# An MLP in two phases, with the down projection as seven products of combined quarters

## The chip, the core and the metric

The kernel runs on one NeuronCore of a Trainium2 chip. TensorE multiplies matrices, VectorE and ScalarE work element by element, GpSimd does almost nothing here, and SyncE (SP) issues nearly all DMAs, in order, to 16 DMA engines. Each engine works through its own queue in order and waits on semaphores of the others. The metric is the device time of one execution in microseconds (us). The median of three runs before is 2216.18 us (2214.98 to 2216.64).

## What is computed

One decoder layer over 512 tokens of width 2048: token mixing, cross-attention, then a squared-ReLU MLP with hidden width 8192, and a final RMSNorm. The change touches the last two:

```python
hn = rmsnorm(h, norm_mlp_g[l])
h = h + jnp.einsum('blf,fd->bld', jnp.square(jax.nn.relu(jnp.einsum('bld,df->blf', hn, w_up[l]))), w_down[l])
...
return rmsnorm(h, norm_final_g)
```

All inputs are float32.

## The kernel before

Activations lie transposed: a tile holds 128 channels on partitions and the 512 tokens along the row. The residual `h` is 16 such tiles, `hres`. Each float32 product is made of three TensorE products of a shorter float type: an operand x is split into xh (ScalarE copies it with rounding) and xl = x - xh (VectorE subtracts), and `mm3` adds wh xh, wh xl and wl xh into one PSUM bank.

`wload` fetches eight 128x128 weight blocks by one DMA into `wr` (two buffers) and splits them into `wh` and `wl` (three buffers each). `gemm` runs `mm3` over these blocks. In all of this the weight block is the stationary operand (128x128) and the activations move (512 columns).

The MLP runs over eight chunks of 1024 hidden channels. In a chunk eight up tiles are made (16 blocks deep; VectorE applies ReLU and the norm's factor, ScalarE squares, `split` makes `uh` and `ul`). Then 16 output tiles of down are made, each eight blocks deep, and VectorE adds each to its tile of `hres`. Per chunk this is 8 x 16 x 3 = 384 matmuls up and 16 x 8 x 3 = 384 matmuls down.

At the end the squares of `hres` are summed over partitions on TensorE, `rsqrt` runs eleven small VectorE instructions, the result is spread over partitions on TensorE, and 16 scalings on VectorE are followed by 16 writes of the output.

A scheduler sets the order on each engine from the program's order and from priorities; what stands inside `urgent()` comes as early as its inputs allow in the scheduler's reckoning. The pools' buffers decide when a load may start: a DMA into a buffer waits for the last reader of what was in it.

Of the kernel before, what the change touches and what calls it, by code (L numbers as in the profile page):

```python
# [56 lines left out]
def trunk(ctx, tc, A, out):  # L57
# [866 lines left out]

    pd = pool("mlp", side="left", reuse_waits="tile")
    for f in range(0, DFF // P, FC):
        UH, UL = [], []
        for j in range(FC):
            o = psum_mm()
            gemm(o, A["w_up"][f + j], list(range(KT)), XH_, XL_)  # L930
            with urgent():
                r = pd.tile([P, L], F32, name="r", bufs=2)
                V.scalar_tensor_tensor(r, o, 0.0, rsh2, op0=OP.max, op1=OP.mult)  # L933
                S.activation(r, r, AF.Square)  # L934
                h, l = split(r, f"uh{j}", f"ul{j}", pd, [P, L])
            UH.append(h)
            UL.append(l)
# [7 lines left out]
    o = rs_psum(sumsq(hres), 1.0 / D, EPS)  # L945
    for c in range(KT):
        t = pd.tile([P, L], F32, name="ot", bufs=4)
        V.scalar_tensor_tensor(t, hres[c], vc("fin_g", c), o, op0=OP.mult, op1=OP.mult)
        Q.dma_start(out[:, c], t)

# [84 lines left out]
```

## Time and profile before

| | before |
|---|---|
| median of three runs | 2216.18 us |
| the profiled execution's own time | 2214.54 us |
| its span, first to last instruction | 2212.8 us |
| TensorE busy | 2169.6 us, 98% |
| VectorE busy | 1168.3 us, 53% |
| ScalarE busy | 778.2 us, 35% |
| DMA, mean | 110 GB/s |
| mean granted clock of TensorE | 0.994 of 2.4 GHz |

Busy time of TensorE counts overlapping matmuls once, and says that something was in flight, not how fast. What a matmul costs is read from the starts of successive ones. The chain of waits goes back from the last instruction, at each step to what released it. In the views by line, a line that helpers use (`mm3`, `split`, `wload`) holds the work of several stages, which the tile names tell apart.

### The profile page before, as it was taken

How to read it: one execution, taken by the hardware profiler on the slowest of the kernel's cores; microseconds unless marked ns; L12 is line 12 of the kernel's file. 1: busy time of each engine (PE TensorE's matmuls, PEld its weight loads, DVE VectorE, ACT ScalarE, POOL GpSimd, SP SyncE). 2: the span in 40 equal slices, each digit the busy share in tenths (PEclk: the TensorE clock that was granted, in tenths of full speed). 3: DMA queues.
4: the chain of work that ended last, by engine and by line, in shares of the span. 5: the costliest groups of instructions: out<-in, count | busy, mean ns of one | idle time of the engine just before them, and what ended most of it. 6: DMA issues, size and time to landing. Idle time of an engine off the chain costs nothing.

```text
span 2212.8 us, 24813 instructions
## 1 busy us (share of the span) xinstructions
PE 2169.6 (98%) x9672; PEld 1757.9 (79%) x9672; DVE 1168.3 (53%) x1761; ACT 778.2 (35%) x1131; POOL 18.1 (1%) x57
## 2 busy tenths in 40 slices
PE   8999999999999999999999999999999999999996
PEld 6777777656988788888888888888888888888885
DVE  7999999976766663333333333333333333333344
ACT  6565543546435543222223212222212222222231
POOL 0000000000000000000000000000000000000000
PEclk9999999999999999999999999999999999999998
DMA  8553326433433133323332333332332332332332
GB/s 295 169 164 122 111 78 213 132 92 100 145 100 105 48 119 96 95 95 98 101 98 95 96 95 99 100 97 96 96 96 98 101 97 96 95 96 99 101 96 95
DMA packets 82134, 244.40 MB, mean 110 GB/s; under 512 B 10448, under 2 KB 12112, under 8 KB 82016
## 3 DMA queue, kind: packets, MB, share of 16 engines
q1 hardware_dynamic: 79808, 235.47, 33.7%
q0 software_dynamic: 2208, 7.34, 0.9%
q8 instruction: 76, 1.25, 0.2%
q14 instruction: 42, 0.34, 0.0%
HBM read 229.12 MB, written 13.13 MB: 109 GB/s over the span
## 4 chain that ended last, share of the span: by engine, by line
PE 92%; DMA 3%; DVE 3%; ACT 1%; issue 1%; SPq 0%; ACTq 0%; DVEq 0%
PE mm L129 29%; PE mm L131 29%; PE mm L130 29%; PE acc L480 1%; PE acc L791 1%; PE two L762 1%; DMA wr<-in_w_xk 1%; DVE wl L125 1%; PE sm L786 1%; DVE al L151 1%; ACT wh L124 0%; DMA ss<-in_pool_w 0%; DVE hc L540 0%; DMA sB<-in_xtok 0%; PE two L422 0%
## 5 line engine op out<-in xcount | busy, mean ns | idle before, releaser
L124 ACT ACTIVATE wh<-wr 128x1024 fp32r<-128x1024 f32 (+1 forms) x424 | 411.7, 971 | 1235.0 <-PE mm L130 1146.0
L129 PE MATMUL mm<-ah,wh 128*128 128x512 f32 (+1 forms) x1920 | 742.9, 387 | 5.3 <-ACT cs L438 2.4
L131 PE MATMUL mm<-ah,wl 128*128 128x512 f32 (+1 forms) x1920 | 741.8, 387 | 0.2 <-DVE wl L125 0.2
L130 PE MATMUL mm<-al,wh 128*128 128x512 f32 (+1 forms) x1920 | 740.1, 385 | 0.0
L125 DVE TENSOR_TENSOR wl<-wr,wh 128x1024 fp32r<-128x1024 f32 (+1 forms) x424 | 471.4, 1113 | 303.6 <-ACT wh L124 300.9
L129 PEld LDWEIGHTS mm<-ah,wh 128*128 128x128 f32 x1920 | 361.8, 188 | 83.0 <-issue 5.4
L131 PEld LDWEIGHTS mm<-ah,wl 128*128 128x128 f32 x1920 | 361.6, 188 | 76.7 <-issue 4.7
L130 PEld LDWEIGHTS mm<-al,wh 128*128 128x128 f32 x1920 | 361.9, 188 | 74.1 <-issue 5.4
L129 PE MATMUL mm<-uh,wh 128*128 128x512 f32 x1024 | 398.8, 389 | 0.0
L130 PE MATMUL mm<-ul,wh 128*128 128x512 f32 x1024 | 397.5, 389 | 0.0
L131 PE MATMUL mm<-uh,wl 128*128 128x512 f32 x1024 | 397.5, 389 | 0.0
L942 DVE TENSOR_TENSOR h<-mm,h 128x512 f32<-128x512 f32 x128 | 88.5, 692 | 415.9 <-PE mm L131 415.9
L131 PEld LDWEIGHTS mm<-uh,wl 128*128 128x128 f32 x1024 | 192.3, 188 | 39.8
L130 PEld LDWEIGHTS mm<-ul,wh 128*128 128x128 f32 x1024 | 192.3, 188 | 39.8
L129 PEld LDWEIGHTS mm<-uh,wh 128*128 128x128 f32 x1024 | 192.4, 188 | 39.7
L933 DVE SCALAR_TENSOR_TENSOR r<-mm,rsx 128x512 f32<-128x512 f32 x64 | 44.3, 692 | 208.7 <-PE mm L131 207.9
L540 DVE SCALAR_TENSOR_TENSOR hc<-pad,wdw,hc 128x512 f32<-128x512 f32 x120 | 86.1, 746 | 0.0
L723 DVE TENSOR_TENSOR h<-mm,h 128x512 f32<-128x512 f32 x64 | 43.9, 688 | 32.4 <-PE mm L131 31.8
L146 DVE TENSOR_TENSOR ul<-r,uh 128x512 fp32r<-128x512 f32 x64 | 44.3, 693 | 1.4 <-ACT uh L145 1.4
L188 DVE TENSOR_TENSOR sqa<-sqa,sqt 128x512 f32<-128x512 f32 x60 | 41.1, 685 | 5.0 <-ACT sqt L187 4.9
L145 ACT ACTIVATE uh<-r 128x512 fp32r<-128x512 f32 x64 | 40.5, 633 | 2.1
L934 ACT ACTIVATE r<-r 128x512 f32<-128x512 f32 x64 | 39.5, 618 | 0.8 <-DVE r L933 0.8
(305 smaller groups left out, 1166.9 us busy)
## 6 DMA issues: line engine op xcount, KB each, us to landing
wr<-in_w_up SPq DMA_DIRECT2D x128, 512.0 KB, 3.7
wr<-in_w_down SPq DMA_DIRECT2D x128, 512.0 KB, 3.7
wr<-in_w_in SPq DMA_DIRECT2D x56, 512.0 KB, 3.9
wr<-in_w_out SPq DMA_DIRECT2D x64, 256.0 KB, 3.0
h<-in_xT SPq DMA_DIRECT2D x16, 256.0 KB, 6.2
wr<-in_w_xk SPq DMA_DIRECT2D x8, 512.0 KB, 3.8
wr<-in_w_xv SPq DMA_DIRECT2D x8, 512.0 KB, 3.7
wr<-in_w_xq SPq DMA_DIRECT2D x8, 512.0 KB, 3.8
```

What stands on the lines that cost most here:

```text
L124: S.activation(h, r, AF.Copy)
L125: V.tensor_tensor(l, r, h.bitcast(F32), op=OP.subtract)
L129: T.matmul(o, wh, xh, start=start, stop=False)
L130: T.matmul(o, wh, xl, start=False, stop=False)
L131: T.matmul(o, wl, xh, start=False, stop=stop)
L145: S.activation(h, src, AF.Copy)
L146: V.tensor_tensor(l, src, h.bitcast(F32), op=OP.subtract)
L188: V.tensor_tensor(acc, acc, sq, op=OP.add)
L540: V.scalar_tensor_tensor(hc[c], hps[c][:, o:o + L], w, hc[c], op0=OP.mult, op1=OP.add)
L723: V.tensor_tensor(hres[c], o, hres[c], op=OP.add)
L933: V.scalar_tensor_tensor(r, o, 0.0, rsh2, op0=OP.max, op1=OP.mult)
L942: V.tensor_tensor(hres[c], o, hres[c], op=OP.add)
```

## The change

The MLP now has two phases: all 64 up tiles first, then all of down. Down uses a scheme with seven products in place of eight for 2x2 blocks (Strassen's, in Winograd's form). In a chunk of 1024 hidden channels the activations are a matrix of 512 tokens by 1024, cut into four quarters of 256 x 512, and the weights a matrix of 1024 x 2048, cut into four quarters of 512 x 1024. Four of the seven activation operands and four of the seven weight operands are sums or differences of quarters.

- `up_pair` makes two up tiles, builds the combinations of their quarters in `z` (seven operands, four of them made by VectorE), splits all seven at once and writes them to DRAM (`ud`). The residual is transposed to tokens on partitions (`h_block`, 64 transposes on TensorE), and four of the seven accumulators start from it (`xd`, also by way of DRAM).
- `down_product` loads one of the seven activation operands (`u_load`, three buffers), makes combinations of weight quarters in place where needed (line 1025), splits them into `w2h` and `w2l` (lines 1027 and 1028, five buffers each), and runs 48 matmuls in four tiles of twelve. Now the tokens are the stationary operand and the weights move. Results go into four PSUM banks, two sets in turn, and VectorE adds them to one of seven accumulators `x1` to `x7` in SBUF (line 1048).
- Weight quarters arrive as two tiles of 128x2048 each (`raw2`, eight buffers, one chunk's worth).
- In the last chunk `merge` forms the outputs from the accumulators, and `down_tail` norms them along the row. The output is written as tokens by channels.

```diff
-    for f in range(0, DFF // P, FC):
-        UH, UL = [], []
-        for j in range(FC):
-            o = psum_mm()
-            gemm(o, A["w_up"][f + j], list(range(KT)), XH_, XL_)
...
-        for c in range(KT):
-            o = psum_mm()
-            gemm(o, A["w_down"][c][:, f:f + FC], list(range(FC)), UH, UL)
             with urgent():
-                V.tensor_tensor(hres[c], o, hres[c], op=OP.add)
...
+    for j in range(2):
+        sl = slice(j * L, (j + 1) * L)
+        for b in range(2):
+            xs = pz.tile([P, 8, 256], F32, name="z", bufs=2).rearrange("p a n -> p (a n)")
+            x2, x3, x4, x7 = (xs[:, i * L:(i + 1) * L] for i in range(4))
+            S.activation(x2, h_block(b, 0, j), AF.Copy)
+            S.activation(x3, h_block(b, 1, j), AF.Copy, scale=-1.0)
+            S.activation(x7, h_block(b + 2, 1, j), AF.Copy)
+            V.tensor_tensor(x4, x7, h_block(b + 2, 0, j), op=OP.subtract)
+            for i, x in ((2, x2), (3, x3), (4, x4), (7, x7)):
+                Q.dma_start(xd[i, b][:, sl], x)
...
+    def up_pair(q, pr):
+        z = pz.tile([P, 8, 256], F32, name="z", bufs=2)
+        for i in range(2):
+            o = psum_mm()
+            gemm(o, A["w_up"][8 * q + 2 * pr + i], list(range(KT)), XH_, XL_)
+            with urgent():
+                r = pz.tile([P, L], F32, name="r", bufs=2)
+                V.scalar_tensor_tensor(r, o, 0.0, rsh2, op0=OP.max, op1=OP.mult)
+                S.activation(z[:, 1:3] if i else z[:, 0:8:7], r.rearrange("p (a b) -> p a b", a=2), AF.Square)
+        with urgent():
+            V.tensor_tensor(z[:, 3], z[:, 7], z[:, 2], op=OP.add)
+            V.tensor_tensor(z[:, 4], z[:, 3], z[:, 0], op=OP.subtract)
+            V.tensor_tensor(z[:, 5], z[:, 0], z[:, 7], op=OP.subtract)
+            V.tensor_tensor(z[:, 6], z[:, 4], z[:, 1], op=OP.subtract)
+            h, l = split(z[:, :7], "zh", "zl", pz, [P, 7, 256], bufs=2)
+            for i, t in enumerate((h, l)):
+                if pr == 0:
+                    ud[q, i] = dr.tile([P, 7, 4, 256], F32, name=f"ud{q}{i}")
+                Q.dma_start(ud[q, i][:, :, pr], t.bitcast(F32))
...
+            uu = u_load(q, idx)
+            wt = {}
+            for j in range(2):
+                for a in range(2):
+                    r = [x[j][:, 2 * a:2 * a + 2] for x in (w,) + tuple(t for c in comb for t in c)]
+                    for c in range(0, len(r) - 1, 3):
+                        V.tensor_tensor(flat(r[c + 1]), flat(r[c + 2]), flat(r[c + 3]), op=OP.subtract)
+                    h, l = w_tile("h"), w_tile("l")
+                    S.activation(flat(h), flat(r[0]), AF.Copy)
+                    V.tensor_tensor(flat(l), flat(r[0]), flat(h).bitcast(F32), op=OP.subtract)
+                    wt[j, a] = h, l
+        o = psum_two() + [psum_sm(), psum_sm()] if sets[0] else [psum_mm(), psum_mm(), psum_mm(), psum_acc()]
...
+            for p in range(2):
+                uh, ul = (t[:, 2 * a + p, b * P:(b + 1) * P] for t in uu)
+                T.matmul(o[2 * j + b], uh, h[:, p], start=a == 0 and p == 0, stop=False)
+                T.matmul(o[2 * j + b], uh, l[:, p], start=False, stop=False)
+                T.matmul(o[2 * j + b], ul, h[:, p], start=False, stop=a == 1 and p == 1)
...
+                        V.tensor_tensor(x, x, o[2 * j + b], op=OP.add)
...
+        down_product(q, 6, b22, (), (3,))
...
+        down_product(q, 0, b11, (), (1,))
+        down_product(q, 4, b22, ((b12, b12, b11), (b22, b22, b12)), (6,))
+        if last:
+            merge(2, 2, 1, OP.add)
+            merge(6, 6, 1, OP.add)
...
+        down_product(q, 5, b11, ((b11, b22, b11),), (7,))
...
+        down_product(q, 2, b22, ((b22, b22, b21),), (4,))
...
+        down_product(q, 3, b12, (), (3, 7) if last else (5,))
...
+        down_product(q, 1, b21, (), (2,), last)
```

Three places in the order of the instructions. On VectorE, inside the MLP of before, a split of weights and an accumulation of a finished output tile take turns:

```order
L125 TENSOR_TENSOR wl<-wr,wh 128x1024 [waits DMAHW3_49,Activation_49]
L942 TENSOR_TENSOR h_3412<-mm,h_3412 128x512 [waits PE_49]
L125 TENSOR_TENSOR wl<-wr,wh 128x1024 [waits DMAHW4_49,Activation_49]
L942 TENSOR_TENSOR h_3414<-mm,h_3414 128x512 [waits PE_49]
L125 TENSOR_TENSOR wl<-wr,wh 128x1024 [waits DMAHW5_49,Activation_49]
L942 TENSOR_TENSOR h_3416<-mm,h_3416 128x512 [waits PE_49]
```

On VectorE after the change, at the start of the second down chunk (`wq_12436` and `wq_12438` are its weight tiles for the first product, `wq_12444` a quarter already combined once for the third, `x_11961` the accumulator of the last product of the chunk before):

```order
L1028 TENSOR_TENSOR w2l<-wq_12436,w2h 128x1024 [waits DMAHW2_49,PE_49,Activation_49]
L1025 TENSOR_TENSOR wq_12436<-wq_12436,wq_12444 128x1024 [waits DVE_49]
L1028 TENSOR_TENSOR w2l<-wq_12436,w2h 128x1024 [waits Activation_49]
L1048 TENSOR_TENSOR x_11961<-x_11961,two 128x512 [waits PE_49] x2
L1025 TENSOR_TENSOR wq_12436<-wq_12436,wq_12444 128x1024 [waits DVE_49]
L1028 TENSOR_TENSOR w2l<-wq_12438,w2h 128x1024 [waits DMAHW5_49,Activation_49]
L1025 TENSOR_TENSOR wq_12438<-wq_12438,wq_12446 128x1024 [waits DVE_49]
```

The accumulation of a finished product now stands between splits and combinations for a later one, and the combinations are new.

On VectorE at the change from up to down: the last rows of an up stage before, ahead of the first accumulation of down (`r` is the eviction of an up tile, `ul` its low part):

```order
L933 SCALAR_TENSOR_TENSOR r<-mm,rsx 128x512 [waits DVE_49,PE_49]
L125 TENSOR_TENSOR wl<-wr,wh 128x1024 [waits DMAHW6_49,DVE_49,Activation_49]
L146 TENSOR_TENSOR ul_9910<-r,uh_9909 128x512 [waits Activation_49]
L942 TENSOR_TENSOR h_3386<-mm,h_3386 128x512 [waits PE_49]
L125 TENSOR_TENSOR wl<-wr,wh 128x1024 [waits DMAHW7_49,DVE_49,Activation_49]
```

and after, at the one place where the phase changes:

```order
L961 SCALAR_TENSOR_TENSOR r<-mm,rsx 128x512 [waits PE_49]
L964 TENSOR_TENSOR z<-z 128x256 [waits Activation_49]
L965 TENSOR_TENSOR z<-z 128x256 [waits DVE_49]
L967 TENSOR_TENSOR z<-z 128x256 [waits DVE_49]
L147 TENSOR_TENSOR zl<-z,zh 128x1792 [waits DMAHW2_49,Activation_49]
L1028 TENSOR_TENSOR w2l<-wq_11865,w2h 128x1024 [waits Activation_49]
```

Before, the weights of the first down tiles are split ahead of the last up tile's eviction or soon behind it; now the first split of down stands behind all work on the last pair of up tiles.

On SP, before, the loads of `w_down` follow those of `w_up` and wait for nothing but their two buffers:

```order
L119 DMA wr<-in_w_up 128x1024 [waits DMAHW0_49,DVE_49]
L119 DMA wr<-in_w_up 128x1024 [waits DMAHW1_49,DVE_49]
L119 DMA wr<-in_w_down 128x1024 [waits DMAHW2_49,DVE_49]
L119 DMA wr<-in_w_down 128x1024 [waits DMAHW3_49,DVE_49]
L119 DMA wr<-in_w_down 128x1024 [waits DMAHW4_49,DVE_49]
```

and after, at the change of phase (`wq_11873` to `wq_11879` are two of the four weight quarters, `u_11964` and `u_11966` the activations of the second product):

```order
L972 DMA ud_11428<-zh 896x1x256 [waits Activation_49]
L972 DMA ud_11430<-zl 896x1x256 [waits DMAHW1_49,DVE_49]
L1077 DMA wq_11873<-in_w_down 128x2048 [waits DMAHW2_49,PE_49]
L1077 DMA wq_11875<-in_w_down 128x2048 [waits PE_49]
L1077 DMA wq_11877<-in_w_down 128x2048 [waits DMAHW4_49,PE_49]
L1077 DMA wq_11879<-in_w_down 128x2048 [waits DMAHW5_49,PE_49]
L1010 DMA u_11964<-ud_7522 128x1024 [waits DMAHW7_49,DMAHW6_49,DMAHW0_49]
L1010 DMA u_11966<-ud_7524 128x1024
```

The four quarter tiles and the second product's activations stand behind the last write of the up phase. The first product's weights and activations (`wq_11865` to `wq_11871`, `u_11881`) are loaded earlier, in the up phase.

## Rows read from the trace of the kernel before

**Rows 1.** The page: span, busy time (share) by engine, chain of waits.

```profile
span 2212.8 us, 24813 instructions
PE 2169.6 (98%) x9672; PEld 1757.9 (79%) x9672; DVE 1168.3 (53%) x1761; ACT 778.2 (35%) x1131; POOL 18.1 (1%) x57
...
PE 92%; DMA 3%; DVE 3%; ACT 1%; issue 1%; SPq 0%; ACTq 0%; DVEq 0%
PE mm L129 29%; PE mm L131 29%; PE mm L130 29%; PE acc L480 1%; PE acc L791 1%; PE two L762 1%; DMA wr<-in_w_xk 1%; DVE wl L125 1%; PE sm L786 1%; DVE al L151 1%; ACT wh L124 0%; DMA ss<-in_pool_w 0%; DVE hc L540 0%; DMA sB<-in_xtok 0%; PE two L422 0%
```

**Rows 2.** MLP windows: us, busy PE, PEld, DVE, ACT, POOL; granted clock, DMA share, GB/s.

```profile
1000.00:1100.00 100.00, 100.00 (x443) 82.88 (x442) 35.38 (x38) 26.04 (x30) 0.00 (x0) 1.00 0.32 96
...
1900.00:2000.00 100.00, 100.00 (x443) 82.87 (x442) 35.10 (x37) 23.54 (x25) 0.00 (x0) 1.00 0.32 98
```

**Rows 3.** Timeline in the last down stage: start us, duration us, engine, line, operation.

```profile
2150.02 0.39 PE L129 MATMUL mm<-uh,wh 128*128 128x512 f32 x1
...
2160.90 0.39 PE L129 MATMUL mm<-uh,wh 128*128 128x512 f32 x1
```

**Rows 4.** Timeline of the tail: the last accumulation and the last scaling.

```profile
2189.66 0.69 DVE L942 TENSOR_TENSOR h<-mm,h 128x512 f32<-128x512 f32 x1 [3.30 <-PE mm L131]
...
2208.42 0.75 DVE L948 SCALAR_TENSOR_TENSOR ot<-h,vec,sm 128x512 f32<-128x512 f32 x1 [0.31 <-DVE ot L948]
```

**Rows 5.** Timeline of transposes: eight among matmuls, four in the tail.

```profile
721.12 1.04 PE L906 MATMUL sm<-ident,pr 128*128 128x128 f32 x8
721.91 0.36 PE L130 MATMUL two<-kl,qh 128*128 128x256 f32 x1
...
2196.11 1.09 PE L172 MATMUL sm<-ident,rs 128*128 128x128 f32 x4 [2.32 <-DVE rs L167]
```

**Rows 6.** Groups by line and form (busy us, mean ns); then starts on VectorE.

```profile
L125 DVE TENSOR_TENSOR wl<-wr,wh 128x1024 fp32r<-128x1024 f32 x336 | 411.4, 1224 | 294.7 <-ACT wh L124 292.2 <-DMA ss<-in_onehot 1.5 <-DMA rvd<-sB 0.8
L942 DVE TENSOR_TENSOR h<-mm,h 128x512 f32<-128x512 f32 x128 | 88.5, 692 | 415.9 <-PE mm L131 415.9
L166 DVE SCALAR_TENSOR_TENSOR rq_t<-rq_t,rq_v 128x4 f32<-128x4 f32 x27 | 4.3, 160 | 0.6
L298 DVE TENSOR_TENSOR cpr<-t,scr 128x256 f32<-128x256 f32 x1 | 0.4, 426 | 0.0
L124 ACT ACTIVATE wh<-wr 128x1024 fp32r<-128x1024 f32 x336 | 356.3, 1061 | 1132.3 <-PE mm L130 1087.7 <-DMA wr<-in_w_in 16.5 <-DMA wr<-in_w_xv 11.1
L145 ACT ACTIVATE uh<-r 128x512 fp32r<-128x512 f32 x64 | 40.5, 633 | 2.1
...
329.29 1.22 DVE L125 TENSOR_TENSOR wl<-wr,wh 128x1024 fp32r<-128x1024 f32 x1
330.42 2.73 DVE L540 SCALAR_TENSOR_TENSOR hc<-pad,wdw,hc 128x512 f32<-128x512 f32 x4
...
339.69 0.69 DVE L125 TENSOR_TENSOR wl<-wr,wh 128x512 fp32r<-128x512 f32 x1
340.29 2.74 DVE L540 SCALAR_TENSOR_TENSOR hc<-pad,wdw,hc 128x512 f32<-128x512 f32 x4
```

**Rows 7.** DMA, 378 to 388 us (rates by 0.25 us, queue), then loads from 1000.

```profile
GB/s 402 418 393 393 377 410 385 385 393 393 393 385 377 393 393 385 369 393 410 352 401 361 360 369 385 393 402 426 393 377 401 344 320 254 74 25 16 0 0 0
q1 hardware_dynamic: 1650, 2.99, 81.0%
...
wr<-in_w_up SPq DMA_DIRECT2D x7, 512.0 KB, 3.6
```

**Rows 8.** Windows around a gap: us, TensorE busy, granted clock, DMA share, GB/s.

```profile
61.00:62.00 1.00, 0.00 (x0) 1.00 0.98 295
62.00:63.00 1.00, 0.85 (x2) 0.50 0.42 164
...
65.00:66.00 1.00, 1.00 (x5) 0.79 0.41 94
66.00:67.00 1.00, 1.00 (x6) 1.00 0.46 103
```

More of the change, by code (lines that the diff above doesn't have):

```diff
@@ L68, in trunk @@
     cp = pool("consts")
-    wp = pool("weights")
-    ap = pool("acts")
+    wa = ExitStack()
+    wp = wa.enter_context(tc.tile_pool(name="weights", bufs=1))
+    ap = wa.enter_context(tc.tile_pool(name="acts", bufs=1))
     ps = pool("psum", space=PSUM)
@@ L702, in trunk @@
     rc.close()
-    hp_ = pool("h", side="right", reuse_waits="tile")
+    hx = ExitStack()
+    hp_ = hx.enter_context(tc.tile_pool(name="h", bufs=1, side="right", reuse_waits="tile"))
     hres = []
@@ L922, in trunk, with h_block @@
     sc_.close()
-    pd = pool("mlp", side="left", reuse_waits="tile")
-    for f in range(0, DFF // P, FC):
-        UH, UL = [], []
-        for j in range(FC):
+    zc = ExitStack()
+    pz = zc.enter_context(tc.tile_pool(name="up", bufs=1, side="left", reuse_waits="tile"))
+    xd = {(i, b): dr.tile([P, 1024], F32, name=f"xd{i}{b}") for i in (2, 3, 4, 7) for b in range(2)}
+    def h_block(b, dn, j):
+        o = psum_sm()
+        for i in range(4):
+            T.transpose(o[:, i * P:(i + 1) * P], hres[8 * dn + 4 * j + i][:, b * P:(b + 1) * P], ident)
+        return o
@@ L946, in trunk @@
[L946 to L949, printed above, removed]
+                S.activation(z[:, 1:3] if i else z[:, 0:8:7], r.rearrange("p (a b) -> p a b", a=2), AF.Square)
[9 more added lines that the diff above has]
+                Q.dma_start(ud[q, i][:, :, pr], t.bitcast(F32))
@@ new lines, in trunk, with acc_tile, flat @@
+    NC_ = DFF // P // FC
+    for q in range(NC_):
+        for pr in range(4):
+            up_pair(q, pr)
+    zc.close()
+    wa.close()
+    p2 = pool("down", side="left", reuse_waits="tile")
+    acc = {}
+    def acc_tile(i):
+        t = p2.tile([P, 2, 2, L], F32, name=f"x{i}")
+        if (i, 0) in xd:
+            for b in range(2):
+                Q.dma_start(t[:, b].rearrange("p j n -> p (j n)"), xd[i, b])
+        acc[i] = t
+    def flat(t):
+        return t.rearrange("p a n -> p (a n)")
@@ new lines, in trunk, with raw2, u_load @@
+    for i in (3, 1, 6, 7):
+        acc_tile(i)
+    raws, us, ws = [0], [0], [0]
+    def raw2():
+        n = raws[0] % 8
+        raws[0] += 1
+        return (p2a if n < 4 else p2).tile([P, 4, L], F32, name=f"wq{n}")
+    def u_load(q, idx):
+        n = us[0] % 3
+        us[0] += 1
+        uu = []
+        for i in range(2):
+            t = (p2 if n else p2a).tile([P, 4, 256], F32R, name=f"u{n}{i}")
+            Q.dma_start(t.bitcast(F32), ud[q, i][:, idx])
+            uu.append(t)
+        return uu
@@ new lines, in trunk, with down_tail @@
+    ssq = cp.tile([P, 8], F32, name="sx")
+    rf = cp.tile([P, 4], F32, name="rf")
+    fin = {}
+    def down_tail(t, ids):
+        with urgent():
+            if t:
+                fin["g"] = flat(raw2())
+                Q.dma_start(fin["g"], A["fin_row"].to_broadcast([P, D]))
+                fin["sq"] = raw2().rearrange("p (a b) n -> p a (b n)", a=2)
+            for b in range(2):
+                k = 4 * t + 2 * b
+                for i in range(2):
+                    S.activation(fin["sq"][:, i], flat(acc[ids[i]][:, b]), AF.Square, accum_out=ssq[:, k + i:k + i + 1])
+                s1 = rf[:, 2 * t + b:2 * t + b + 1]
+                V.reduce_sum(s1, ssq[:, k:k + 2], axis=AX.X)
+                rsqrt(s1, s1, 1.0 / D, EPS)
+                for i in range(2):
+                    x = flat(acc[ids[i]][:, b])
+                    V.scalar_tensor_tensor(x, x, s1, fin["g"][:, 1024 * i:1024 * i + 1024], op0=OP.mult, op1=OP.mult)
+                    r0 = 256 * t + P * b
+                    Q.dma_start(out[r0:r0 + P, 1024 * i:1024 * i + 1024], x)
@@ L952, in _bucket @@
+    for q in range(NC_):
+        down_chunk(q, q == NC_ - 1)
 def _bucket(dist):
@@ L1028 @@
          for k, a in arrays.items()}
-    out = nc.dram_tensor("out", (P, KT, L), F32, kind="ExternalOutput").ap()
+    out = nc.dram_tensor("out", (L, D), F32, kind="ExternalOutput").ap()
     with _tile.TileContext(nc, schedule_with_timeline_sim=True) as tc:
```

66 lines of the change are left out of this document (58 added, 8 removed).

## The prediction

> **What bounds the kernel now.** I read the busy table first, then the chain of waits, then the stage windows, then single instructions. The busy table gives TensorE 98% of the span, VectorE 53%, ScalarE 35%; the chain is 92% TensorE, and its three largest lines are the three matmuls of `mm3` [rows 1]. A busy TensorE alone proves little, since matmuls overlap. The windows say more: two stretches of 100 us in the MLP, 900 us apart, hold the same 443 matmul starts each at full granted clock, while VectorE is busy 35 us and the DMA engines are at a share of 0.32 [rows 2]. From the matmul that starts at 2150.02 to the one at 2160.90 lie 48 matmuls, so one costs 10.88 / 48 = **0.2267 us**, and so far nothing waits in between [rows 3]. So the MLP, which ends with the accumulation that starts at 2189.66 us, is a count of matmuls. The rest is a tail of 2212.8 - 2189.66 = 23.1 us after the last matmul [rows 4].
>
> **What is removed.** Down has 64 x 16 x 3 = 3072 matmuls now, and 8 chunks x 7 products x 48 = 2688 after. Operands change sides (tokens are loaded as the stationary 128x128, weights move 512 wide), but shape and type of each matmul stay, so I keep the pitch: 384 x 0.2267 = **-87.1 us**.
>
> **What is added on TensorE.** 64 transposes of `hres` near the start of the up phase. Eight such transposes take 721.12 to 721.91, 0.10 us each; four in the tail take 1.09, 0.27 each, at half clock [rows 5]. Between 6.4 and 17.4 us; I take **+6.4**, because the first row stands, as these will, among dense matmuls. ScalarE and VectorE evict them beside TensorE.
>
> **VectorE in the down phase.** This is the closest call. One chunk asks VectorE for 28 subtractions that make `w2l`, 16 that combine weight quarters, all 128x1024, and 28 accumulations of 128x512 from PSUM. The same work has 1.224 us and 0.692 us now, and back to back it starts every 1.13 us (329.29 to 330.42) and 0.60 us (339.69 to 340.29) [rows 6]. So 44 x 1.13 + 28 x 0.60 = 66.5 us at the low price, 44 x 1.224 + 28 x 0.692 = 73.2 at the high one, against 336 x 0.2267 = 76.2 us of TensorE. It fits, with 3 to 10 us per chunk to spare. Within the chunk it doesn't fit everywhere. A product is 10.88 us of TensorE. The one with two combinations needs 12 x 1.13 + 4 x 0.60 = 16.0 us of VectorE (high: 17.5), each of the two with one combination 11.4 (12.6), the other four 6.9 (7.7). The three heavy ones follow each other and overdraw by 5.1 + 0.5 + 0.5 = 6.1 us (high: 6.6 + 1.7 + 1.7 = 10.0). The cover is the five `w2h`/`w2l` pairs: VectorE can stand four tiles of 12 matmuls, 4 x 2.72 = 10.9 us, ahead, and the light products restore the lead. If that cover is gone, 6 to 10 us per chunk come out in the open. ScalarE has 28 x 1.06 = 30 us per chunk and never decides. Steady chunks: between 0 and 9 us in all, I take **+2**.
>
> **DMA in the down phase.** A chunk loads eight weight quarters of 1.05 MB and fourteen u tiles of 0.52 MB, 15.7 MB in 76.2 us, 206 GB/s. The trace holds 385 to 410 GB/s over several microseconds when the queue is full [rows 7], so half the engines' time is enough. In the order, the load of a u tile waits for the product three before it, hence has two products (21.8 us) to land. The up phase writes 1.8 MB per pair of up tiles in 1 KB pieces. In the tightest stretch, 1650 packets took 81% of 16 engines for 10 us, 0.079 us each at about 2 KB; at that price 1792 pieces cost 8.8 us on 16 engines, and four weight loads 6.8 more (0.32 of 21.8), in a pair's 21.8 us. No charge.
>
> **The change of phase.** Here the trace before shows nothing like it, so I add up the chain. When the last up matmul ends (call it T0), the first down product still lacks its `w2h` and `w2l`, since their buffers lie where the up phase's tiles were, and on VectorE and ScalarE they queue behind the last pair: eviction 0.69, square 0.63, three 256-wide combinations 3 x 0.43, `zh` 1792 wide (1.06 + 1.5 x 0.43 = 1.70), `zl` (1.22 + 1.5 x 0.53 = 2.02), the first `w2l` 1.22 [rows 6]. With six handoffs of some 0.08 this is 8.0 us of idle TensorE. After such a gap it also comes back slower: in the gap before 62 us TensorE did nothing, the clock then stood at 0.50 until about 65.5 us and at 1.00 from 66 us [rows 8]. Half of 3.5 us is 1.8 us. So the first product ends at T0 + 8.0 + 10.9 + 1.8 = T0 + 20.7.
>
> The second needs its u tiles. On SP these stand behind the last `zl` write (issued at T0 + 6.7) and four quarters: 0.9 + 4 x 1.05 + 1.05 = 6.2 MB at 0.39 MB/us is 15.8 us. A 512 KB load lands after 3.6 us [rows 7], 2.3 more than its bytes take, so u is there at T0 + 24.8: a second gap of 4.1 us, and 1.8 for the clock. The second product ends at T0 + 37.5. The third needs the PSUM banks of the first, whose accumulation stands on VectorE behind 17 combinations and splits that begin with the first quarter's landing (T0 + 14.1): 17 x 1.13 + 3.6 for the four accumulations and what lies between puts it at T0 + 37. Both chains agree: product three starts near T0 + 38 where T0 + 21.8 would be free. **+17 us**. Lower bound 13 (the u tiles early, VectorE's chain alone, a little cheaper); upper bound 31, if the queue moves 205 GB/s, what the chunk asks on average, instead of 390.
>
> The Trainium skill, "DMA: Bandwidth & Descriptors", section "Bandwidth", says that a 1 MB load runs at 341 GB/s and that HBM limits a core to some 358 GB/s. The trace disagrees, with 385 to 410 GB/s; at the page's 341 an estimate for the 6.2 MB is 18.2 us instead of 15.8, and the sum would be 2.4 us longer. The measurement decides.
>
> **The end.** In the last chunk VectorE also merges accumulators, 14 x 1.13 to 1.22 = 16 to 17 us, and adds one product twice. But no next chunk's combinations wait behind it, so most of it fits in the room that leaves: between 0 and 9 us, I take **+1.5**. After the last matmul the order leaves on VectorE one accumulation (0.7), 48 small instructions of 0.16 us, 0.18 with their handoffs (8.6), and eight scalings 1024 wide. Those took 0.75 us at 512 [rows 4, 6]; by the same step they are 1.2 each (9.6). With 3.6 us from the last scaling to the end, as now (2208.42 + 0.75 to 2212.8), 22.5 us against 23.1. **0**, between -4 and +4.
>
> **Sum.** -87.1 + 6.4 + 2 + 17 + 1.5 + 0 = -60.2 us. On the profiled execution, whose span is 2212.8 and whose own time is 2214.54 us, this gives 2154.3; the median of the runs is 1.64 us above it, so **2156 us**. The low ends of all terms give -87.1 + 6.4 + 0 + 13 + 0 - 4 = -71.7, 2144; the high ends -87.1 + 17.4 + 9 + 31 + 9 + 4 = -16.7, 2200, but they hardly come together.
>
> **Rivals.** (a) *Loads run late in every chunk.* The combination that opens the next chunk's quarters stands in VectorE's queue four or five rows behind the split that frees the buffer it is loaded into. If each such wait costs TensorE 2 to 4 us, eight chunks cost 16 to 32: 2172 to 2188. For it: SP's queue is in order, and a late wait on it holds all loads behind. Against it: two products of time for each load.
> (b) *The lead is lost: slower than before.* The accumulations that wait for TensorE stand between the splits on VectorE's in-order queue. Should VectorE enter the heavy products without its four tiles, their overdraw is open in each chunk: at the high price 10.0 us, times eight 80 us, 2236. It decides from 60.2 / 8 = 7.5 us per chunk on; at the low price, 6.1, the result is 2205, still faster. For it: VectorE at 88% to 96% of TensorE's time. Against it: the order has the splits of a product ahead of the accumulation of the one before. The Trainium skill, "TensorE: Matmul & The Clock Gate", section "HAM oscillation", says that matmul bursts with waits between them keep returning the engine to half clock. The trace agrees for single gaps, with 0.50 after the gap above [rows 8].
> (c) *A matmul of this kind costs more with the sides swapped,* so that the seven products don't save an eighth. From 60.2 / 2688 = 0.022 us more per matmul on nothing is left: about 2216. Against it: shape and types are the same.
> (d) *The change of phase is mostly hidden,* by loads that start earlier than I read: below 2144.
>
> **How the numbers follow.** Forecast 0.62, (a) 0.19, (b) 0.07, (c) 0.03, (d) 0.09. The range 2142 to 2192 holds the forecast, (a), and half of (d); outside are (b), (c) and the rest of (d), with tails of the others somewhat under 0.2. A measurement of this kernel can tell some 0.2% (4.4 us) from no change. Faster: forecast, (a), (d) and the low price of (b), 0.91; same 0.03; slower 0.06.
>
> **What would show it.** In the profile after: matmul pitch 0.2267 in the down phase; a gap of about 8 us on TensorE released by `w2l`, a second one of some 4 us released by the u load, clock 0.50 behind each; VectorE busy 85% to 97% in the down phase with TensorE full from the second chunk on; a tail of 20 to 26 us. Wrong would be gaps of TensorE released by `w2l` in each chunk at the product with two combinations (b), or VectorE waiting for weight loads (a), or a second gap over 10 us (the upper bound of the change of phase).

## Result and the profile after

The changed kernel takes 2161.06 us (median of 4 runs, 2158.28 to 2163.11) against 2216.07 of the kernel before: ratio **0.9752**, interval 0.9735 to 0.9768, some 55 us faster. The prediction was 2156, between 2142 and 2192. The profiled execution takes 2159.74 us with a span of 2158.0, 54.8 less than in [rows 1].

The page of the changed kernel, to be read beside [rows 1]: span, busy time by engine, chain of waits by engine.

```profile
span 2158.0 us, 24750 instructions
...
PE 2101.5 (97%) x9340; PEld 1692.6 (78%) x9340; DVE 1538.5 (71%) x2201; ACT 906.3 (42%) x1219; POOL 18.1 (1%) x57
...
PE 89%; DVE 4%; DMA 4%; ACT 2%; issue 1%; SPq 0%; DVEq 0%; ACTq 0%
```

TensorE has 332 instructions fewer on record, VectorE 370 us more work, and the chain is still TensorE's. Windows of the changed kernel, columns as in [rows 2]: a steady stretch as long as a chunk, and the one with the most work for VectorE, which begins 12 us ahead of the last chunk.

```profile
1588.00:1665.00 77.00, 77.00 (x337) 62.93 (x336) 67.17 (x71) 30.54 (x30) 0.00 (x0) 1.00 0.57 205
...
2050.00:2127.00 77.00, 77.00 (x337) 62.90 (x336) 76.10 (x81) 29.92 (x29) 0.00 (x0) 1.00 0.33 113
```

TensorE never stops in either. But 77 us hold 337 matmul starts, where [rows 2] would give 341, and VectorE, with 67.2 us in the steady stretch, has 76.1 in the second: there it has 0.9 us left (2.6 in the last 77 us of down, 2062 to 2139, where it is busy 74.4).

At the change of phase TensorE stops twice. Its timeline in the changed kernel (start, duration, operation, idle time ahead and what ended it):

```profile
1505.81 0.39 PE L132 MATMUL mm<-ah,wl 128*128 128x512 f32 x1
1511.75 1.22 PE L1037 MATMUL two<-w2h,u 128*128 128x512 f32 x2 [5.55 <-ACT w2h L1027]
1514.00 0.79 PE L1038 MATMUL two<-w2l,u 128*128 128x512 f32 x1 [1.03 <-DVE w2l L1028]
...
1527.10 0.40 PE L1039 MATMUL sm<-w2h,u 128*128 128x512 f32 x1
1531.56 0.76 PE L1037 MATMUL mm<-w2h,u 128*128 128x512 f32 x1 [4.06 <-DMA u<-ud]
...
1544.91 0.39 PE L1037 MATMUL two<-w2h,u 128*128 128x512 f32 x1
```

And the same stretch in windows:

```profile
1512.00:1518.70 6.70, 5.67 (x13) 3.99 (x14) 5.35 (x5) 3.52 (x5) 0.00 (x0) 0.50 1.00 307
1518.70:1527.00 8.30, 8.30 (x35) 6.64 (x35) 5.63 (x5) 3.15 (x3) 0.00 (x0) 0.95 1.01 422
...
1531.50:1536.00 4.50, 4.44 (x11) 3.50 (x12) 4.50 (x5) 0.00 (x0) 0.00 (x0) 0.50 1.03 411
```

The last up matmul starts at 1505.81; one pitch later is T0, 1506.04. The first gap has two parts: 5.55 us until ScalarE's first w2h, on which two matmuls start at T0 + 5.7, and 1.03 us until VectorE's first w2l, whose matmul starts at 1514.00, T0 + 7.96. The second gap is 4.06 us and ends with the u load. Behind each the granted clock is 0.50 (1.2 GHz), in windows of 6.7 and 4.5 us. The third product (1544.91) starts at T0 + 38.9. The first w2l, the second gap and the start of the third product were forecast to within a microsecond. The rest of this document is mostly on three things that were not.

### The profile page after: what moved, and what is told of

Read it like the earlier page. It is cut to its first block, busy times and chain, and to the rows that moved or that the text cites. A ratio compares the mean times of both kernels' runs of the same rounds, so it can differ in the third digit from the quotient of the medians.

```text
span 2158.0 us, 24750 instructions
## 1 busy us (share of the span) xinstructions
PE 2101.5 (97%) x9340; PEld 1692.6 (78%) x9340; DVE 1538.5 (71%) x2201; ACT 906.3 (42%) x1219; POOL 18.1 (1%) x57
## 4 chain that ended last, share of the span: by engine, by line
PE 89%; DVE 4%; DMA 4%; ACT 2%; issue 1%; SPq 0%; DVEq 0%; ACTq 0%
PE mm L130 19%; PE mm L132 19%; PE mm L131 19%; PE mm L1037 4%; PE mm L1038 4%; PE mm L1039 4%; PE two L1038 2%; PE sm L1038 2%; PE two L1037 2%; PE sm L1037 2%; PE sm L1039 2%; PE two L1039 2%; PE acc L481 1%; PE acc L1037 1%; PE acc L1038 1%; PE acc L1039 1%
## 5 line engine op out<-in xcount | busy, mean ns | idle before, releaser
L125 ACT ACTIVATE wh<-wr 128x1024 fp32r<-128x1024 f32 (+1 forms) x296 | 275.8, 932 | 586.7 <-PE mm L131 486.1
L126 DVE TENSOR_TENSOR wl<-wr,wh 128x1024 fp32r<-128x1024 f32 (+1 forms) x296 | 314.0, 1062 | 183.6 <-ACT wh L125 183.3
L1027 ACT ACTIVATE w2h<-wq 128x1024 fp32r<-128x1024 f32 x224 | 237.6, 1062 | 364.9 <-PE two L1039 92.9
L1028 DVE TENSOR_TENSOR w2l<-wq,w2h 128x1024 fp32r<-128x1024 f32 x224 | 270.1, 1219 | 64.6 <-ACT w2h L1027 64.2
L1025 DVE TENSOR_TENSOR wq<-wq,wq 128x1024 f32<-128x1024 f32 x128 | 153.7, 1217 | 7.6 <-DMA wq<-in_w_down 7.3
L1037 PE MATMUL mm<-w2h,u 128*128 128x512 f32 x336 | 132.0, 395 | 4.1 <-DMA u<-ud 4.1
L1038 PE MATMUL mm<-w2l,u 128*128 128x512 f32 x336 | 132.7, 395 | 0.0
L1039 PE MATMUL mm<-w2h,u 128*128 128x512 f32 x336 | 131.6, 392 | 0.0
L1037 PE MATMUL two<-w2h,u 128*128 128x512 f32 x224 | 88.6, 399 | 5.5 <-ACT w2h L1027 5.5
L1038 PE MATMUL two<-w2l,u 128*128 128x512 f32 x224 | 89.2, 398 | 1.0 <-DVE w2l L1028 1.0
L1039 PE MATMUL two<-w2h,u 128*128 128x512 f32 x224 | 88.4, 395 | 0.0
L1039 PE MATMUL sm<-w2h,u 128*128 128x512 f32 x224 | 87.5, 391 | 0.0
L1037 PE MATMUL sm<-w2h,u 128*128 128x512 f32 x224 | 87.1, 392 | 0.0
```

The costliest lines, as they stand in the source:

```text
L125: S.activation(h, r, AF.Copy)
L126: V.tensor_tensor(l, r, h.bitcast(F32), op=OP.subtract)
L1025: V.tensor_tensor(flat(r[c + 1]), flat(r[c + 2]), flat(r[c + 3]), op=OP.subtract)
L1027: S.activation(flat(h), flat(r[0]), AF.Copy)
L1028: V.tensor_tensor(flat(l), flat(r[0]), flat(h).bitcast(F32), op=OP.subtract)
L1037: T.matmul(o[2 * j + b], uh, h[:, p], start=a == 0 and p == 0, stop=False)
```

## Experiments

All times below are medians; the kernel before took 2215.2 to 2215.8 beside them.

### 1. Every third down product is slower

Timeline of the changed kernel: the last matmuls of four products in a row.

```profile
1577.74 0.39 PE L1039 MATMUL sm<-w2h,u 128*128 128x512 f32 x1
...
1588.62 0.40 PE L1039 MATMUL acc<-w2h,u 128*128 128x512 f32 x1
...
1599.83 0.39 PE L1039 MATMUL sm<-w2h,u 128*128 128x512 f32 x1
...
1610.75 0.39 PE L1039 MATMUL acc<-w2h,u 128*128 128x512 f32 x1
```

48 matmuls lie between each two. The first and the third stretch are 10.88 and 10.92 us (0.2267 and 0.2275 a matmul), the middle one is 11.21 (0.2335; 11.20 and 0.2333 in the later ones of its kind). It is the product whose stationary tiles are buffer u0, and so it goes on in all chunks: 19 of 56 products. Shape, type, clock and order are the same; what differs is where u0 lies. By the program's allocation u0 starts at byte 221152 of a partition, u1 at 164416, the moving tiles w2h at 98880.

Two kernels moved the start addresses. The first puts 32 bytes behind u0:

```
+        if us[0] == 1:
+            G.memset(p2a.tile([P, 8], F32, name="off"), 0.0)
```

> In the changed kernel every third down product, the one whose stationary operand is buffer u0, runs at 0.2333 us a matmul instead of 0.2267. u0 starts at byte 221152 of a partition, 32 past a multiple of 64; u1, u2 and all w2h and w2l start at multiples of 64. Here 32 bytes are put behind u0, so that it starts at 221120, a multiple of 64, and nothing else of the down products moves. Theory (the offset of one operand against the other sets the pitch): all products at 0.2267, 18 or 19 products x 48 x 0.0066 = 6 us less, about 2155. Rival (the place: u0 lies on the right side of the memory among the raw quarters): 0.2333 stays in every third product, 2161.

Measured: 2159.89 us; u0's products at 0.2325, the others at 0.2267. The second puts 32 bytes ahead of w2h and as many ahead of u1:

```
+        if not ws[0]:
+            ws[0] = 1
+            G.memset(p2.tile([P, 8], F32, name="offw"), 0.0)
```

> The counterpart: w2h and w2l, the moving operand of every down product, are shifted by 32 bytes, u0 stays at 32 past a multiple of 64, u1 and u2 at multiples of 64. Theory (one operand's offset against the other's): now u0's products run at 0.2267 and those of u1 and u2 at 0.2333: 37 products x 0.32 us more, 19 x 0.32 less, about 6 us more than the changed kernel, 2167. Rival of the place: as the changed kernel, every third at 0.2333, 2161. Rival of the moving operand's own offset: all at 0.2333, 2173. Rival of the stationary operand's own offset: as the changed kernel, 2161.

Measured: 2172.49 us; all products take 11.15 to 11.19 us, 0.2323 to 0.2331 a matmul. So the place was not it alone (u1 and u2 became slow when w2h moved by 32 bytes and they by 64), and the theory had the wrong modulus: u0 stayed slow where it agreed modulo 64. A third kernel gave the three buffers three offsets against w2h:

```
+        if us[0] in (2, 3):
+            G.memset(p2.tile([P, 16 * us[0] + 32], F32, name=f"off{n}"), 0.0)
...
+        if us[0] == 1:
+            G.memset(p2a.tile([P, 104], F32, name="off"), 0.0)
```

> With u0 moved to a multiple of 64 bytes its products still took 0.2325 us a matmul (0.2333 before the move, 0.2267 for u1 and u2). Counted modulo 512, the moving tiles w2h and w2l start at 64, u1 and u2 at 64 too, u0 at 480 in the changed kernel and at 448 after the move. Here u0 goes to 64 (416 bytes behind it), u1 to 320 (256 further than w2), u2 to 128 (64 further). Theory (the pitch is 0.2267 only where both operands start alike modulo 512): u0's products at 0.2267, those of u1 and u2 at 0.2325 or more; down longer by 37 x 0.28 less 19 x 0.32, about 2165. Rival of the place (u0's side of the memory is slower by itself): u0 stays at 0.2325 and u1 and u2 at 0.2267, 2160. Rival modulo 256: u0 and u1 at 0.2267, u2 at 0.2325, 2160.

Measured: 2162.60 us. Its timeline, last matmuls of four products in a row; the three stretches between them are u2, u0 and u1:

```profile
1778.81 0.39 PE L1043 MATMUL sm<-w2h,u 128*128 128x512 f32 x1
...
1790.00 0.39 PE L1043 MATMUL acc<-w2h,u 128*128 128x512 f32 x1
...
1800.91 0.39 PE L1043 MATMUL sm<-w2h,u 128*128 128x512 f32 x1
...
1811.79 0.39 PE L1043 MATMUL acc<-w2h,u 128*128 128x512 f32 x1
```

u2 (64 bytes off) takes 11.19 us, u0 (0 off) 10.91, u1 (256 off) 10.88. The rival of modulo 256 holds and the two others fall.

The kernel before had such matmuls too, in the projection `w_xo` behind the attention. Its stationary blocks `wh` start at 32 modulo 256, its moving tiles `oh` and `ol` at 160. Two matmuls of it, from the kernel before, with 48 starts from the one to the other:

```profile
783.97 0.39 PE L129 MATMUL mm<-oh,wh 128*128 128x512 f32 x1
...
795.17 0.39 PE L131 MATMUL mm<-oh,wl 128*128 128x512 f32 x1
```

These are 11.20 us, 0.2333 a matmul, at the same shape and type as in [rows 3]. Over all kernels, start addresses modulo 256:

| kernel, tile | stationary | moving | us a matmul |
|---|---|---|---|
| before: wh and ah | 32 | 32 | 0.2267 |
| before: wh and oh | 32 | 160 | 0.2333 |
| changed: u1, u2 | 64 | 64 | 0.2267 |
| changed: u0 | 224 | 64 | 0.2333 |
| first: u0 | 192 | 64 | 0.2325 |
| second: u1 / u0 | 128 / 224 | 96 | 0.2331 / 0.2323 |
| third: u0, u1 / u2 | 64 / 128 | 64 | 0.2267 / 0.2333 |

The rule that fits all rows: equal modulo 256 is fast, and the differences tried (32, 64, 128 and 160) cost some 3%. Why, no run shows.

### 2. One long up tile

One up tile takes 14.6 us where all others take 10.9. Windows of the changed kernel around it:

```profile
860.00:890.00 30.00, 30.00 (x136) 24.86 (x135) 16.93 (x20) 10.81 (x12) 0.00 (x0) 1.00 1.01 364
890.00:900.00 10.00, 6.90 (x30) 5.07 (x29) 5.06 (x7) 4.45 (x4) 0.00 (x0) 1.00 0.62 213
```

ScalarE's waits in it from 860 to 920 us (waited for: us in total, times, longest):

```profile
ACT wh L125 <- DMA wr<-in_w_up: 17.9, 7, 5.1
```

The DMA engines are full (share 1.01) and ScalarE waits for w_up; TensorE then stands 2.6 us for `wh` and 0.5 us for `wl`. On SP the first four quarter tiles (two quarters, 1 MB a tile) stand among the first weight loads and writes of the up phase, at 861 to 869 us, because their buffers are free. The experiment holds them back by a one-element copy that needs a later hidden tile:

```
+    def early_load(k, j):
+        with urgent():
+            t = raw2()
+            V.tensor_copy(t[:, 0, :1], mark[0])
+            Q.dma_start(t, A["w_down"][0, k, k, :, j])
...
+            if q == 4:
+                early_load(1 - pr // 2, pr % 2)
```

> The four 1 MB loads of raw quarters that the changed kernel issues at the very start of the up phase (SP has them among the first weight loads and the writes of combined hidden tiles) are held back to the fifth eighth of the up phase, one per pair. Theory (the up tile of 14.6 us instead of 10.9 near 893 us waits for w_up behind these loads): every up tile takes 10.9, about 3.7 us less, 2157. Rival (the writes in 1 KB pieces of the combined hidden tiles and of the accumulators' start values do it): one long tile stays, 2161.

Measured: 2157.26 us, and no long tile. The same window in this kernel:

```profile
890.00:900.00 10.00, 10.00 (x46) 8.29 (x45) 4.33 (x6) 3.22 (x4) 0.00 (x0) 1.00 0.28 95
```

The loads of the quarters did it; the writes in 1 KB pieces alone do not.

### 3. Do two chains end together at the change of phase?

The prediction said that the late u load costs nothing by itself, since VectorE's chain puts the third product at the same time. The test loads u ahead of the quarters:

```
+                if q == 0 and b is b12:
+                    ready.extend([u_load(0, 6), u_load(0, 0)])
```

> At the change of phase the u tiles of the second product are loaded ahead of the four raw quarters b12 and b21, not behind them. Theory of the prediction (two chains end together: the u load, and VectorE's 17 combinations and splits ahead of the first product's accumulation): the second gap of 4.1 us on TensorE goes, but the quarters land some 2.6 us later and VectorE with them, so product three starts between T0 + 38 and T0 + 41 as before; 2160 to 2164. Rival (the u load alone set it): product three starts near T0 + 33 and the kernel takes about 2155.

Measured: 2161.85 us. TensorE's waits of this kernel from 1500 to 1560 us:

```profile
PE two L1037 <- ACT w2h L1027: 5.5, 1, 5.5
PE mm L1038 <- DVE w2l L1028: 2.3, 1, 2.3
PE two L1037 <- ACT x L1046: 1.6, 1, 1.6
PE two L1038 <- DVE w2l L1028: 1.0, 1, 1.0
```

The wait for u is gone, and waits for VectorE have come in its place. The second is put down to ScalarE (`ACT x`), but that instruction had been done for 0.8 us; VectorE's accumulation of the first product's first tile ends at 1547.67, 0.1 us before the matmul. T0 is 1510.72 here and the third product starts at 1547.77: T0 + 37.1 against T0 + 38.9. Of 4.1 us and a half clock behind it, 1.8 us were to be had in the profiled executions; the medians, 2161.85 and 2161.06, don't tell the two kernels apart. VectorE in the changed kernel says the same: its accumulations of the two tiles that the third product needs first are

```profile
1540.68 0.68 DVE L1048 TENSOR_TENSOR x<-x,two 128x512 f32<-128x512 f32 x1
...
1543.01 0.68 DVE L1048 TENSOR_TENSOR x<-x,two 128x512 f32<-128x512 f32 x1
```

They end at T0 + 35.3 and T0 + 37.7. With VectorE's work in this order an earlier u could have brought the third product forward by 3.6 us at most. The two chains end within a few microseconds of each other.

### 4. How much room VectorE has: rival (b) by dose

Some of the subtractions that make w2l are done twice:

```
                     V.tensor_tensor(flat(l), flat(r[0]), flat(h).bitcast(F32), op=OP.subtract)
+                    if idx in (3, 1):
+                        V.tensor_tensor(flat(l), flat(r[0]), flat(h).bitcast(F32), op=OP.subtract)
```

> In the products that use b12 and b21 plain (two of seven) every subtraction that makes w2l is done twice, so VectorE has 8 more of 128x1024 per chunk, the data are the same. Rival (b) of the prediction by price: if one costs its pitch of 1.13 us, a chunk asks 66.5 + 9.0 = 75.5 of 77.0 us and nothing or little is lost, 2161 to 2169; if it costs its duration of 1.22, a chunk asks 73.2 + 9.8 = 83.0, 6.0 us over, times eight 48, about 2209. Theory: the low price, since VectorE is busy 67.6 us of 77 in a steady chunk of the changed kernel.

> The same in all four products without combinations: 16 more per chunk. At 1.13 us each a chunk asks 66.5 + 18.1 = 84.6 of 77.0 us: 7.6 over, times eight some 61 us, 2222, slower than the kernel before the change. At the duration of 1.22: 92.7, 15.7 over, 126 us, 2287. Rival (VectorE has more room than it shows): under 2200. In the trace TensorE should wait for w2l in every chunk.

Measured: 2184.70 and 2231.24 us. Windows of the kernel with 8 more, a steady stretch and the last chunk:

```profile
1760.00:1840.00 80.00, 78.92 (x342) 63.88 (x342) 77.22 (x83) 29.63 (x28) 0.00 (x0) 1.00 0.56 198
...
2077.00:2154.00 77.00, 68.17 (x287) 54.32 (x286) 77.00 (x82) 26.50 (x27) 0.00 (x0) 0.98 0.24 82
```

and of the one with 16 more:

```profile
1600.00:1700.00 100.00, 94.89 (x405) 75.06 (x404) 100.00 (x105) 36.10 (x34) 0.00 (x0) 1.00 0.51 180
```

With 16 more VectorE is busy all the time and sets the pace. Its rows of 1.21 us start every 1.13:

```profile
1794.99 1.21 DVE L1030 TENSOR_TENSOR w2l<-wq,w2h 128x1024 fp32r<-128x1024 f32 x1
1796.12 1.21 DVE L1025 TENSOR_TENSOR wq<-wq,wq 128x1024 f32<-128x1024 f32 x1
```

The six chunks between the first and the last take 84.7 us on average, from the first matmul of one to that of the next, against 77.0 in the changed kernel; 84.6 was expected at the pitch of 1.13 us and 92.7 at the duration of 1.22. The low price is the true one. Of the 70 us that the kernel loses 21.5 go in the last chunk, which takes 98.2 us against 76.7. It is slower than before (ratio 1.0069, 1.0054 to 1.0084), as rival (b) has it. TensorE waits in the steady chunks, 1.2 us at most each time, for w2h as much as for w2l; its granted clock from 1700 to 2000 us is 0.98. With 8 more the expectation of 0 to 8 us was too low: 23.6 us. More than half of it, 13.4 us, is lost in the last chunk (90.1 us against 76.7); in the window above 287 matmuls start in 77 us against 337. There the merges had left 0.9 us. A steady stretch of 80 us starts 342 where 350 fit, some 1.8 us lost, though VectorE still has 2.8 us there: room that small isn't all usable.

The lead was tested by fewer buffers:

```
-        return p2.tile([P, 2, L], F32R, name=f"w2{hl}", bufs=5)
+        return p2.tile([P, 2, L], F32R, name=f"w2{hl}", bufs=3)
```

> Three w2h and w2l pairs in place of five, so VectorE can stand two tiles of 12 matmuls (5.4 us) ahead of TensorE, not four (10.9). Theory of the prediction (the three heavy products overdraw VectorE by 6.1 us per chunk and the lead covers it): about 1 to 3 us per chunk come into the open, and the accumulations held behind splits add to that: 2169 to 2190, waits of TensorE for w2l at the product with two combinations or the one after. Rival (the accumulators' turn-taking spreads the work and the lead isn't used): no waits, 2161.

Measured: 2165.31 us, 4 more than the changed kernel and less than the theory's 8 to 29. TensorE's waits in this kernel from 1560 us on:

```profile
PE sm L1037 <- ACT w2h L1027: 1.1, 1, 1.1
PE two L1038 <- DVE w2l L1028: 0.9, 1, 0.9
PE mm L1038 <- DVE w2l L1028: 0.2, 1, 0.2
```

Its window in the last chunk, where TensorE is short of 77 us by 2.3 (the chunk takes 80.3 us against 76.7):

```profile
2068.00:2145.00 77.00, 74.72 (x322) 59.70 (x321) 76.55 (x86) 33.84 (x38) 0.00 (x0) 1.00 0.24 82
```

In a steady chunk there is no wait even with two tiles of lead (5.4 us): the prediction's overdraw of 6.1 us per chunk is too high, or its five pairs more than is needed. What is lost lies in the last chunk.

### 5. A version that is faster than both

It takes on the three findings. Up phase: single buffers for the combined hidden tiles; in the memory so won, the four w2h and w2l pairs of the first down product are made before T0. First chunk: products in the order 0, 6, 1, 3, 4, 5, 2, and what it needs first is loaded through the Pool queue. Quarters late, all starts alike modulo 256. Core of the edit:

```
+            if q == 4:
+                early_load(pr // 2, pr % 2)
+            if q == 6:
+                early_split(pr // 2, pr % 2)
...
+                ready.extend([u_load(0, 0), u_load(0, 6, G)])
...
+            down_product(q, 3, b12, ((b12, b12, b11),), (5,))
+            down_product(q, 4, b22, ((b22, b22, b12),), (6,))
```

> A version that takes on what the other runs named. Up phase: one buffer each for the combined hidden tiles, so the four w2h and w2l pairs of the first down product get memory of their own and are made in the seventh eighth of the up phase; the first raw quarters are loaded in the fifth eighth. First chunk: products in the order 0, 6, 1, 3, 4, 5, 2, so that the combinations come late and spread out; the accumulator and u loads that it needs first, and the quarters b21 and b12, go by the Pool queue, which is free, and not behind the last writes on SP. 416 bytes behind u0 so that all stationary and moving tiles start alike modulo 256. Theory: the first gap (8.0 and the half clock) and the second (4.1 and the half clock) go, product three starts near T0 + 22 instead of T0 + 38.9 (17 us), 0.2267 in all products (6 us), no long up tile (3.7 us): 2161 - 27 = 2134, up to 2140 with some waits left. Rival (what is loaded after T0 through the Pool queue comes too late for the second product): a gap of 5 us or more behind the first down product, 2142 or more.

> The same version, but with all loads on SP, where those of the first chunk stand behind the last writes of combined hidden tiles (issued near T0 + 6.7). Theory: the second product needs its u tiles at T0 + 10.9; behind 0.9 MB of writes and 1 MB of accumulator they land at about T0 + 14 to 16, so a gap of 3 to 5 us with a half clock behind it, 3 to 7 us more than with the Pool queue, about 2140. Rival (issue on SP is early enough, the bytes set it): no difference, about 2134.

Measured: 2158.60 and 2159.41 us. All products run at 0.2267 in both, and the first gap is gone, but TensorE's largest waits from 800 us on are, in the first:

```profile
PE mm L1081 <- ACT w2h L1071: 12.1, 1, 12.1
PE mm L130 <- DVE z L967: 6.9, 1, 6.9
```

and in the one on SP:

```profile
PE mm L1081 <- DMA u<-ud: 12.3, 1, 12.3
PE mm L130 <- DVE z L967: 6.8, 1, 6.8
```

Both theories missed. The single z buffer was still in use by the accumulators' start values when the first up tile wanted it (13.2 us without an up matmul from 834 us on, in which 36 transposes run), and the second product's first w2h lay in memory that the last zl write still read. With these in the way, the two kernels can't be told apart. The next version mends both: staging buffers of their own, and another turn of the five pairs.

```
+    px = xc.enter_context(tc.tile_pool(name="x_stage", bufs=1, side="right", reuse_waits="tile"))
...
-        n = ws[0] % 5
+        n = ws[0] if ws[0] < 4 else (ws[0] - 4) % 5
```

> The last version mended at the two places where it waited. The accumulators' start values get two staging buffers of their own, on the right beside hres, so that the first up pairs don't wait for the single buffer of squares; and the second down product's first w2h and w2l pair goes into memory that the first down product frees at T0 + 2.7, not into memory that the last writes of combined hidden tiles hold. Theory: the 13.2 us at 834 us and the 12.1 us (and a half clock) behind the first down product both go, product three starts near T0 + 22 to 25, 2132 to 2138. Rival (the loads by the Pool queue come too late in any case, the wait at the second product was only covered by the other one): a wait of TensorE for u of 5 to 12 us there, 2138 to 2147.

Measured: **2137.98 us** (2134.21 to 2138.56), ratio to the kernel before 0.9642 (0.9628 to 0.9656), 1.1% below the changed kernel. Timeline of this kernel at the change of phase:

```profile
1502.26 0.39 PE L132 MATMUL mm<-ah,wl 128*128 128x512 f32 x1
1502.49 0.39 PE L1079 MATMUL two<-w2h,u 128*128 128x512 f32 x1
...
1524.25 0.39 PE L1079 MATMUL two<-w2h,u 128*128 128x512 f32 x1
```

All waits of TensorE in it from 800 us on:

```profile
PE mm L1080 <- DVE w2l L1070: 1.4, 2, 1.1
PE two L1080 <- DVE w2l L1070: 0.8, 1, 0.8
PE mm L1079 <- ACT w2h L1069: 0.2, 1, 0.2
```

The first down matmul follows the last up matmul after 0.23 us, and the third product starts at T0 + 21.8, the free value. What is left are 2.4 us of waits and the clock behind them. Last, the same kernel with its loads on SP:

> The mended version with all its loads on SP, to tell what the Pool queue is worth there. On SP the u load of the fourth down product, which waits until the first one has read its buffer (T0 + 10.9), stands ahead of two accumulators (2.1 MB) and of the second product's u tiles (1 MB). Theory: 3.7 MB at 0.4 MB/us and 2 us behind T0 + 10.9, so TensorE waits about 11 to 12 us for u at the second product, with half a clock behind it: 12 to 15 us more than with the Pool queue, 2150 to 2153. Rival (the order of the queue doesn't matter, since VectorE's chain ends as late anyway): within 4 us of 2138.

Measured: 2149.88 us, and one wait of TensorE:

```profile
PE mm L1079 <- DMA u<-ud: 12.3, 1, 12.3
```

The theory holds: SP stands at a u load whose buffer the first product still reads, the loads that are needed at once stand behind it, and 12 us go with that. The Trainium skill, "Trainium Kernel Development and Optimization", section "Key Constraints", says that DMAs from the SP, ACT and POOL queues share the same 16 engines, so that several issuers save only the issue time. Here it saved more: the bytes are the same in both kernels, and the second queue is worth 2149.88 - 2137.98 = 11.9 us, because it doesn't stand behind what SP waits for.

## Why the prediction was right, and where it was not

| term | predicted | measured | by |
|---|---|---|---|
| 384 matmuls less | -87.1 | -87.1 | pitch 0.2267 in two products of three |
| u0's products | 0 | +6.3 | 19 x (11.21 - 10.88) |
| transposes | +6.4 | +6.3 | 8 groups of 0.79 |
| loads in the up phase | 0 | +3.7 | 14.6 - 10.9 |
| change of phase | +17 | +17.1 | T0 + 38.9 less T0 + 21.8 |
| steady chunks | +2 | 0 | no wait from 1536.5 us on |
| last chunk | +1.5 | 0 | the same |
| tail | 0 | -4.4 | 18.7 against 23.1 |
| ahead of the MLP | - | +2.0 | first eviction at 817.73, before 815.76 |
| sum | -60.2 | -56.1 | span: -54.8 |

Two pairs of rows overlap: four of the transposes (0.4 us) come ahead of the first eviction, and one of u0's products (0.3) lies in the change of phase. With these taken once, 2.0 us stay without a name. That the first eviction comes 2.0 us later lies, but for those transposes, before anything that the change touches; it lay between 816.0 and 820.5 in all changed kernels run here but the first two of experiment 5. The misses have both signs (+6.3, +3.7 and +2.0 against -4.4 and -3.5), so that the sum came within 5 us is in part luck.

**The matmul count** was right, **"shape and type of each matmul stay, so I keep the pitch"** was not: it is the step that failed, and rival (c) in small. Where stationary and moving tile start differently modulo 256, a matmul costs 0.0066 us more, a third of (c)'s break-even of 0.022; a third of the products have it (experiment 1). The pitch was read in one stage of the kernel before; another stage of it, `w_xo`, had 0.2333 at the same shape and type, so shape and type alone don't set it.

**"No charge" for the loads** was worked out over a pair of up tiles, with the bytes of a steady pair. It failed at the start of the phase, where SP issues 4 MB of raw quarters, the accumulators' start values and w_up together (experiment 2).

**The change of phase** holds in its mechanism: 8.0 us to the first w2l, a second gap of 4.1 until u, half clock behind each (as in [rows 8]), and two chains that end close together (experiment 3). In the sizes two misses cancel in part. TensorE stood still 11.0 us (5.7 + 1.0 + 4.2), not 12.1, because two matmuls on w2h start ahead of the first w2l. The half clock cost 5.8 us, not 3.6: the first product takes 15.6 us with its wait of 1.0, where 11.2 is its time at full clock, and the second 13.35 where 10.88 is. And the chains that the prediction added up end at T0 + 37.5 and T0 + 37, at most 15.7 us behind the free value; it took 38 and 17 without giving a term for the rest. That 17 meets 17.1 so closely is luck. Its queue moved 411 to 422 GB/s against the 390 taken from [rows 7].

**VectorE** holds at the low price: the sum of 66.5 us per chunk stands against 67.2 measured. The cover was larger than needed (three pairs lose 4 us in all). The last chunk's forecast came true, and the loss of 1.5 us didn't come, but only 0.9 us were to spare in the fullest 77 us. The reason given (no next chunk's combinations behind it) carries little there: 13 combinations stand in that window, 17 in the steady one, while 12 merges come in; the text didn't add this up. The high price and with it rival (b) fall, but (b)'s mechanism is there: sixteen subtractions more per chunk, and the kernel is slower than before.

**The tail** was mis-sized in the small instructions. VectorE in the changed kernel:

```profile
2139.28 0.69 DVE L1048 TENSOR_TENSOR x<-x,acc 128x512 f32<-128x512 f32 x1 [0.45 <-PE acc L1039]
2139.89 0.21 DVE L1119 TENSOR_REDUCE rf<-sx 128x1 f32<-128x2 f32 x2
2140.07 0.22 DVE L161 TENSOR_SCALAR rq_v<-rf 128x1 f32<-128x1 f32 x2
...
2142.22 2.48 DVE L1123 SCALAR_TENSOR_TENSOR x<-x,rf,wq 128x1024 f32<-128x1024 f32 x2
...
2151.65 2.48 DVE L1123 SCALAR_TENSOR_TENSOR x<-x,rf,wq 128x1024 f32<-128x1024 f32 x2
```

Two chains stand side by side, so a row of two takes 0.19 us, 0.1 for each where 0.18 was taken for a single chain (that of before starts one every 0.20 us, 2193.82 to 2195.79): 48 of them cost some 4.5 us, not 8.6. The scalings (1.2 each) and the last write (3.9 after them) are as forecast.

**Rivals.** (a) did not come: TensorE has no wait for a load after the second product, though VectorE has three for weight quarters, 3.3 us in all. (d) did not either in this kernel, but the version of experiment 5 shows that it could be made true.

## What to carry to other kernels

A product fewer on the bounding engine is worth its full count only while the other engine's room, read stage by stage, is not used up; the last stage, where merges are added, had 0.9 us of 77 left when the steady ones had 10. At a change of phase add up every chain to the first instruction that is free again: taking away one of two that end close together brought 1.8 us, taking away both, with the first gap, 17. Where equal instructions differ in pitch from buffer to buffer, look at the start addresses of their operands.

## What the runs showed of the hardware

- A 128x512 matmul in this three-term scheme took 0.2267 us where stationary and moving tile start alike modulo 256 bytes of a partition, and 0.2323 to 0.2333 where they differ by 32, 64, 128 or 160.
- VectorE's 128x1024 subtractions cost 1.13 us each when it is kept full, not the 1.22 of their rows: 16 more per chunk left it at 100% busy and made a steady chunk 84.7 us long, 84.6 by that price.
- A DMA queue waits in order: a u load on SP that could not start before T0 + 10.9 held back the loads behind it, and TensorE waited 12.3 us.
